# One kernel, three edits around the modulation vectors: VectorE alone for the second group, in-projections' norm without GpSimd, the first group ahead of most filter spectra

## The chip, the cores and the metric

The kernel runs on one core of a Trainium2 chip. The metric is the device time of one execution in microseconds (us); the median of three executions of the kernel before is 1859.73 us (1854.02 to 1862.49). Five engines matter: TensorE (PE, with its weight loads PEld), VectorE (DVE), ScalarE (ACT), GpSimd (POOL) and SyncE (SP), which issues nearly all of the DMAs.

## The reference, cut to what matters

Two layers of a diffusion transformer over 512 latent tokens and 256 context tokens, model width 1024. Each layer reads six modulation vectors per stream (latent, context), normalises, projects in, runs three kinds of token mixing side by side (Hyena convolution, neighbourhood attention NA, latent attention MLA), projects out, and runs an MLP of width 4096.

```python
def _modulation(cond, w_mod, b_mod):
    m = jax.nn.silu(cond) @ w_mod + b_mod
    return jnp.split(m[:, None, :], 6, axis=-1)
def _adaln(h, g, shift, scale):
    return _rms(h, g) * (1.0 + scale) + shift
for i in range(DEPTH):
    mx = _modulation(c, w_mod[i], b_mod[i])            # latent; mc: the same with c_ctx
    px = _adaln(x, g_norm1[i], mx[0], mx[1]) @ w_in[i]
    ...                                                 # Hyena (filters made from hy_f_*), NA, MLA
    x = x + mx[2] * (mix @ w_out[i])
    x = x + mx[5] * _sqrelu_mlp(_adaln(x, g_norm2[i], mx[3], mx[4]), ...)
```

## The kernel before, in words

Activations are kept feature-major: 128 partitions, eight blocks k of the width, 768 tokens (latent 0 to 511, context 512 to 767). Every product is made of three matmuls, each operand being split into a high and a low part (`split`, lines 134 to 137: the high part by an ACT copy on L136, the low part by a DVE subtraction on L137). Weights of the big GEMMs stream from HBM in blocks of 512 KB through the SP queue into a ring of three raw buffers, and each block is split into `wh` and `wl` (`wblock`; its DMA is L280). A GEMM (L295) works through eight k of an output block m.

Modulation vectors (l, v), v = 0 to 5, are made in two ways. `modulation` does it on PE: eight weight tiles `wm` [128, 1024] of `w_mod`, four matmuls each (L150), a transpose (L158). `modulation_rows` does it without PE: per vector eight items, each a tile `wm` of `w_modr` that is multiplied by the row of activated conditions and summed along the row. In the kernel before POOL multiplies by the context's row (L189), ACT sums that product (L194), and DVE multiplies by the latent's row and sums (L193). Vectors (0,1) and (0,0) are made by `modulation` at the start, (0,2) and (0,4) by `modulation` during layer 0's MLA attention, and (0,3), (0,5) and all six of layer 1 by `modulation_rows` during layer 0's out-projection and MLP (64 items).

The order of work is that of the program, in which generators are woven (`weave` with a rate for each, `fill` for work that is slipped in between matmuls); a scheduler of the framework then moves instructions on each engine's queue, except the DMAs of `w_modr`, which keep their order (`pin`). At run time each engine takes its queue strictly in order. During out-projection and MLP one item of `modulation_rows` is issued per output block m or hidden block; the table `FR` gives the number per hidden block in the first two of the MLP's four groups.

At the start SP loads the inputs, the sixteen `w_mod` tiles and the first weights, while PE also makes the Hyena filters' spectra: L357 and L372 (L335 and L350 after the change) compute the filter network, L392 and L401 its norms, L409 (L387) the transform. The first norm multiplies x by the reciprocal norm `rb` (`norm_x`), then `norm_h` makes the high part on ACT, the full value on DVE (L253) and the low part by a subtraction on POOL (L254). Layer 1 does the same per stream (`norm_stream`, L263 to L266), between the MLA in-projection (L295) and the NA value projection (`na_v`, L131 to L133). Out-projection is L1370, the gated residual add L1059, the split of the next input L1375 and L1376, the sum of squares L216 and L217, its reduction over partitions L224 (PE).

Lines of the kernel after stand 22 lines lower in number from the projection code on (before's L1059 is L1037 there), and the two multiplies of an item are L191.

Of the kernel before, what the change touches and what calls it, by code (L numbers as in the profile page):

```python
# [15 lines left out]
AF = mybir.ActivationFunctionType  # L16
# [20 lines left out]
def r32(ap):  # L37
    return ap.bitcast(F32)
# [3 lines left out]
def kernel(ctx, tc, A, dbg=None, stop=None):  # L42
# [131 lines left out]
    def modulation_rows(lv, cr, p):  # L174

        items = [(l, v, k) for l, v in lv for k in range(KD)]
        W, P = {}, {}
        def item(i):
            return items[i] if 0 <= i < len(items) else None

        for i in range(len(items) + MD + 2):
            if item(i):
                l, v, k = items[i]
                W[i] = p([128, 1024], tag="wm", bufs=3)
                pin(sp.dma_start(W[i], A["w_modr"][l, v, k]))
            if item(i - MD):
                l, v, k = items[i - MD]
                P[i - MD] = p([128, 1024], tag="wmp", bufs=2)
                pool.tensor_tensor(P[i - MD], W[i - MD], cr[:, 1], ALU.mult)  # L189
            if item(i - MD - 1):  # L190
                l, v, k = items[i - MD - 1]  # L191
                pr, w = P.pop(i - MD - 1), W.pop(i - MD - 1)
                dve.scalar_tensor_tensor(w, w, 1.0, cr[:, 0], ALU.mult, ALU.mult, accum_out=mods[:, l, v, k, 0:1])  # L193
                act.activation(pr, pr, AF.Copy, accum_out=mods[:, l, v, k, 1:2])  # L194
            if item(i - MD - 2) and items[i - MD - 2][2] == KD - 1:
                l, v, k = items[i - MD - 2]
                bm = cols[:, l, C_BMOD + v * 8:C_BMOD + v * 8 + 8]
                dve.tensor_add(mods[:, l, v], mods[:, l, v], bm.unsqueeze(2).to_broadcast([128, KD, 2]))
                if v % 3 == 1:
                    gain(l, v // 3)  # L200
            yield
# [37 lines left out]
    def norm_x(xT, rb, nt):
        for k in range(KD):  # L240
            dve.tensor_mul(xT[:, k, :nt], xT[:, k, :nt], rb)
            yield
        yield

    def norm_h(l, n, xT, hh, hl, nt, p):

        streams = [e for e in STREAM if e[1] < nt]
        for k in range(KD):
            t = p([128, nt], tag="sq", bufs=2)
            for s, a, b in streams:  # L250
                g, m = gains[:, l, n, k, s:s + 1], mods[:, l, 3 * n, k, s:s + 1]
                act.activation(hh[:, k, a:b], xT[:, k, a:b], AF.Identity, bias=m, scale=g)
                dve.tensor_scalar(t[:, a:b], xT[:, k, a:b], g, m, ALU.mult, ALU.add)  # L253
            pool.tensor_sub(hl[:, k, :nt], t, r32(hh[:, k, :nt]))  # L254
            yield

    def norm_stream(l, s, rb, xT, hh, hl, p):

        _, a, b = STREAM[s]
        for k in range(KD):  # L260
            t = p([128, NT], tag="sq", bufs=2)[:, a:b]
            g, m = gains[:, l, 0, k, s:s + 1], mods[:, l, 0, k, s:s + 1]
            dve.tensor_mul(xT[:, k, a:b], xT[:, k, a:b], rb[:, a:b])  # L263
            act.activation(hh[:, k, a:b], xT[:, k, a:b], AF.Identity, bias=m, scale=g)
            dve.tensor_scalar(t, xT[:, k, a:b], g, m, ALU.mult, ALU.add)
            pool.tensor_sub(hl[:, k, a:b], t, r32(hh[:, k, a:b]))  # L266


    nw = [0]
# [26 lines left out]
                                  stop=(k == nk - 1 and i == 2))  # L296
                next(fill, None)

    MD = 1
    EA = 8  # L300
    MF, VF = 0.5, 0.4

# [11 lines left out]
    NSB, NPT = 3, 4  # L314
    MB = 4
    EM = 8
    FR = (0, 2)


    kx = [tc.dram_tile([128, 2, 2, 2, 2, 256], F32, name=f"kx{l}") for l in range(DEPTH)]  # L320
# [636 lines left out]
    def mla_attend(l, qrs, qk0, qkd, vd, mh, ml, p):  # L957
# [8 lines left out]
        def heads_in(h):  # L966

            hp, z = divmod(h, 2)
            if z == 0 and hp:
                QK[hp] = p([128, 2, 6, 192], tag="qk", bufs=2)  # L970
                for e, n in ((0, nq), (1, 6)):
                    sp.dma_start(QK[hp][:, e, 0:n], qkd[hp, :, e, 0:n])
            if hp:
                q, k = [QK[hp][:, e, :, 96 * z:96 * z + 96] for e in range(2)]
            else:
                q, k = qk0[z]
            qh, ql = p([96, NT], F32R, tag="qh", bufs=3), p([96, NT], F32R, tag="ql", bufs=3)
# [12 lines left out]
            T[h] = ((qh, ql), (kh, kl))  # L990
# [92 lines left out]
    def mlp(l, xT, hh, hl, rstd, streams, p, tail, fill=iter(())):  # L1083
# [10 lines left out]
        def ff1(c):  # L1094
            nonlocal rb
            ah, al = p([128, 4, n], F32R, tag="ah", bufs=2), p([128, 4, n], F32R, tag="al", bufs=2)
            ts = {}
            for j in range(4):
                f = 4 * c + j
                if f == 0:  # L1100
                    ts = {i: (mm_tile(), wblock(A["w_ff1"][l, i])) for i in range(2)}
                    gemm([ts[0][0], ts[1][0]], [ts[0][1], ts[1][1]], KD, (hh, hl), [rng, rng], fill=early())
                    rb = next(rstd)
                    ts[2] = (mm_tile(),)
                    gemm(ts[2][0], wblock(A["w_ff1"][l, 2]), KD, (hh, hl), rng)
# [14 lines left out]
                for s, a, b in STREAM[:len(streams)]:  # L1120
                    act.activation(r[:, a:b], r[:, a:b], AF.Relu, bias=bb[:, s:s + 1])
                dve.tensor_mul(r, r, r)  # L1122
                split(ah[:, j], al[:, j], r)
                for _ in range(FR[c] if c < 2 else 1):
                    next(fill, None)
            return ah, al

# [31 lines left out]
    def chain(*gs):  # L1159
        for g in gs:  # L1160
            yield from g
# [26 lines left out]
    def x_in():
        for rb in rstd:
            yield  # L1190
        for _ in zip(*[norm_x(xT, rb, NT)] * 3):
            yield
# [16 lines left out]
    sc = Pool("norm0", "right")  # L1209
    rstd = norm_rstd(acc, NT, sc)  # L1210
    fill = spectra()
    weave((x_in(), 1.0), (chain(modulation(0, 1, wmp, ws=wm1), modulation(0, 0, wmp, ws=wm0)), 1.0), fill=(fill, 1.4))
    wmp.close()
    sc.close()
    hp_ = Pool("h0")
    hh, hl = hp_([128, KD, NT], F32R), hp_([128, KD, NT], F32R)
    cp = Pool("c0")
    cqh, cql, ssq = cp([128, 3, NT], F32R), cp([128, 3, NT], F32R), cp([128, 2, 6])
    for _ in norm_h(0, 0, xT, hh, hl, NT, xp):
        pass  # L1220
    xp.close()

    xd = tc.dram_tile([128, KD, S], F32, name="x_spill")
    qkd = [tc.dram_tile([4, 128, 2, 6, 192], F32, name=f"qk_spill{l}") for l in range(DEPTH)]
# [2 lines left out]
    for l in range(DEPTH):  # L1227
# [4 lines left out]
        if l:  # L1232
# [332 lines left out]
```

## Time and profile before

| what | us |
|---|---|
| median of three executions | 1859.73 |
| the profiled execution | 1861.99 |
| its span in the trace | 1860.1 |
| PE busy | 1770.8 (95%) |
| DVE busy | 1227.3 (66%) |
| ACT busy | 807.1 (43%) |
| POOL busy | 339.4 (18%) |

The profiled execution is one execution with the hardware profiler. A busy time is the union of the engine's instructions. A matmul of 512 columns in float32 shows as two records; the number of records in a stretch says how dense PE is, even where its busy time is full.

### The profile page before, as it was taken

Reading aid. Unit: us, or ns where it says so; the run is one execution under the profiler, and the core shown is the slowest. Engines: PE = TensorE matmul, PEld = TensorE weight load, DVE = VectorE, ACT = ScalarE, POOL = GpSimd, SP = SyncE. Lnnn points to the kernel's source line nnn. Section 1 sums busy time; section 2 is a strip of 40 time slices with the busy share of each in tenths; the row PEclk is TensorE's granted clock in tenths of the full one; section 3 lists DMA queues with packets and bytes.
Section 4 is the critical chain, followed back from the end, with each engine's and each line's share of the span. In section 5 each row is a group of like instructions: output and inputs, shape, how many; then the busy total and the mean of one; then the engine's idle time right before and its main releaser. Section 6 shows DMA issues by size and latency. Waiting matters only on the chain. (4 is left out here: it accounts for less than half of the span.)

```text
span 1860.1 us, 27267 instructions
## 1 busy us (share of the span) xinstructions
PE 1770.8 (95%) x10794; PEld 1504.4 (81%) x10794; DVE 1227.3 (66%) x2111; ACT 807.1 (43%) x1355; POOL 339.4 (18%) x265
## 2 busy tenths in 40 slices
PE   6899988899998999999999999899899999999999
PEld 2688877666686878888888888789677799999997
DVE  5866876766668876665666447887876665555554
ACT  3433425566644643334333224554566652333231
POOL 1523321200043433233322000530300000000000
PEclk9999998999998999999999999899999999999999
DMA  9123423151243333333332222363040023223332
GB/s 339 60 85 134 161 95 101 42 207 56 100 160 126 114 136 130 120 114 136 113 136 102 69 68 88 96 202 132 24 177 24 24 93 100 91 91 95 98 91 79
DMA packets 73246, 205.07 MB, mean 110 GB/s; under 512 B 12540, under 2 KB 24589, under 8 KB 71840
## 3 DMA queue, kind: packets, MB, share of 16 engines
q1 hardware_dynamic: 71520, 198.10, 31.0%
q0 software_dynamic: 1600, 5.24, 0.8%
q8 instruction: 85, 1.39, 0.3%
q14 instruction: 41, 0.34, 0.1%
HBM read 181.30 MB, written 21.23 MB: 109 GB/s over the span
## 5 line engine op out<-in xcount | busy, mean ns | idle before, releaser
L295 PE MATMUL mm<-t,wh 128*128 128x512 f32 (+1 forms) x2496 | 495.2, 319 | 1.9 <-DVE t L1059 1.3
L295 PEld LDWEIGHTS mm<-t,wh 128*128 128x128 f32 x2496 | 373.2, 190 | 38.0 <-issue 2.4
L136 ACT ACTIVATE wh<-wr 128x1024 fp32r<-128x1024 f32 (+2 forms) x176 | 184.6, 1050 | 415.8 <-PE mm L295 394.4
L295 PE MATMUL mm<-t,wl 128*128 128x512 f32 (+1 forms) x1248 | 298.1, 317 | 0.0
L189 POOL TENSOR_TENSOR wmp<-wm,t 128x1024 f32<-128x1024 f32 x64 | 169.5, 2655 | 485.8 <-DMA wm<-in_w_modr_dram 308.8
L137 DVE TENSOR_TENSOR wl<-wr,wh 128x1024 fp32r<-128x1024 f32 (+2 forms) x176 | 228.0, 1296 | 37.3 <-ACT wh L136 33.8
L295 PE MATMUL mm<-ah,wh 128*128 128x512 f32 (+1 forms) x768 | 231.4, 355 | 4.1 <-DVE t L1059 3.5
L295 PE MATMUL mm<-al,wh 128*128 128x512 f32 (+1 forms) x768 | 233.5, 359 | 0.0
L295 PE MATMUL mm<-ah,wl 128*128 128x512 f32 (+1 forms) x768 | 232.0, 356 | 0.0
L1059 DVE SCALAR_TENSOR_TENSOR t<-mm,mods,t 128x512 f32<-128x512 f32 x216 | 135.9, 657 | 134.3 <-PE mm L295 127.5
L295 PEld LDWEIGHTS mm<-t,wl 128*128 128x128 f32 x1248 | 194.7, 189 | 16.5
L193 DVE SCALAR_TENSOR_TENSOR wm<-wm,t 128x1024 f32<-128x1024 f32 x64 | 91.0, 1426 | 102.7 <-POOL wmp L189 102.7
L295 PEld LDWEIGHTS mm<-ah,wh 128*128 128x128 f32 x768 | 126.7, 188 | 28.5 <-DVE t L1059 3.4
L295 PEld LDWEIGHTS mm<-ah,wl 128*128 128x128 f32 x768 | 127.6, 188 | 22.4
L295 PEld LDWEIGHTS mm<-al,wh 128*128 128x128 f32 x768 | 126.4, 188 | 20.2
L194 ACT ACTIVATE wmp<-wmp 128x1024 f32<-128x1024 f32 x64 | 67.9, 1060 | 149.8 <-POOL wmp L189 149.8
L137 DVE TENSOR_TENSOR al<-relu,ah 128x768 fp32r<-128x768 f32 (+1 forms) x64 | 68.2, 1066 | 37.1 <-ACT ah L136 37.1
L447 DVE TENSOR_REDUCE mmx<-mm 128x1 f32<-128x768 f32 (+1 forms) x80 | 67.7, 847 | 32.1 <-PE mm L133 31.5
L452 ACT ACTIVATE msb<-mm,mmx,qrs 128x768 f32<-128x768 f32 (+1 forms) x80 | 72.2, 903 | 25.3 <-DVE mmx L449 21.3
L1370 PE MATMUL mm<-t,wh 128*128 128x512 f32 x320 | 78.1, 358 | 1.6 <-DVE t L1059 1.6
L1023 ACT ACTIVATE mpt<-mm 128x768 f32<-128x768 f32 (+1 forms) x80 | 57.5, 725 | 49.7 <-PE mm L1022 49.6
L136 ACT ACTIVATE ah<-relu 128x768 fp32r<-128x768 f32 (+1 forms) x64 | 47.3, 739 | 63.4 <-DVE relu L1122 63.3
(311 smaller groups left out, 2990.1 us busy)
## 6 DMA issues: line engine op xcount, KB each, us to landing
wr<-in_w_ff_dram SPq DMA_DIRECT2D x128, 512.0 KB, 3.5
wm<-in_w_modr_dram SPq DMA_DIRECT2D x64, 512.0 KB, 4.4
wm<-in_w_mod_dram SPq DMA_DIRECT2D x32, 512.0 KB, 8.0
wr<-in_w_in_t_dram SPq DMA_DIRECT2D x18, 512.0 KB, 3.8
qk<-qk_spill SPq DMA_DIRECT2D x9, 576.0 KB, 6.2
qk_spill<-upk SPq DMA_DIRECT2D x12, 384.0 KB, 3.0
kx<-kk POOLq DMA_DIRECT2D x16, 256.0 KB, 2.5
wr<-in_w_in_qk_dram SPq DMA_DIRECT2D x8, 512.0 KB, 4.0
```

What stands on the lines that cost most here:

```text
L136: act.activation(hi, src, AF.Copy)
L137: dve.tensor_sub(lo, src, r32(hi))
L189: pool.tensor_tensor(P[i - MD], W[i - MD], cr[:, 1], ALU.mult)
L193: dve.scalar_tensor_tensor(w, w, 1.0, cr[:, 0], ALU.mult, ALU.mult, accum_out=mods[:, l, v, k, 0:1])
L194: act.activation(pr, pr, AF.Copy, accum_out=mods[:, l, v, k, 1:2])
L295: pe.matmul(out_[:, po:po + b - a], wk[wx], mk[mx][:, a:b], start=(k == 0 and i == 0), stop=(k == nk - 1 and i == 2))
L447: dve.tensor_reduce(mx, src, AX.X, ALU.max, negate=True)
L452: act.activation(sb[:, h, :n], src[:, h, :n], AF.Exp, bias=mx[:, h:h + 1], scale=1.0 if scale is None else scale[:, h:h + 1], accum_out=sm ...
L1023: act.activation(pt[:, 0:nkt, qt * 128:(qt + 1) * 128], tt[:, :nkt * 128].rearrange("p (c q) -> p c q", q=128), AF.Copy)
L1059: dve.scalar_tensor_tensor(xT[:, m, a:b], t[:, a:b], mods[:, l, v, m, s:s + 1], xT[:, m, a:b], ALU.mult, ALU.add)
L1370: pe.matmul(t[:, a:b], ws[wx], half[mx][:, k % 4, a:b], start=(k == ks[0] and i == 0), stop=(k == 7 and i == 2))
```

## The change

`modulation_rows` keeps its weight tiles and their DMAs, but both products are made by DVE, with two `scalar_tensor_tensor` with accumulation per item; weights are loaded two items ahead (`MD` 2) instead of one. Vector (0,3) moves from the out-projection into layer 0's MLA attention, with conditions loaded and activated for it once more; `FR` becomes one item per hidden block from the second group on, none in the first; the three `next(fill)` behind the out-projection go. The ring `qk` of the MLA attention has one buffer instead of two, in both layers. `norm_x` and `norm_h` go; both layers use `norm_stream`, which multiplies on DVE, applies gain and shift on ACT in place, and splits with ACT and DVE. At the start the first modulation is woven with half as much spectral work per step as the spectra's former rate (0.5 instead of 1.4), and `rb` is made behind it.

```diff
+        for i in range(MD):
+            weights(i)
+        for i, (l, v, k) in enumerate(items):
+            weights(i + MD)
+            w, junk = W.pop(i), p([128, 1024], tag="wmp")
+            for s in range(2):
+                dve.scalar_tensor_tensor(w if s else junk, w, 1.0, cr[:, s], ALU.mult, ALU.mult,
+                                         accum_out=mods[:, l, v, k, s:s + 1])
-                pool.tensor_tensor(P[i - MD], W[i - MD], cr[:, 1], ALU.mult)
...
-                dve.scalar_tensor_tensor(w, w, 1.0, cr[:, 0], ALU.mult, ALU.mult, accum_out=mods[:, l, v, k, 0:1])
-                act.activation(pr, pr, AF.Copy, accum_out=mods[:, l, v, k, 1:2])
...
     def norm_stream(l, s, rb, xT, hh, hl, p):
         _, a, b = STREAM[s]
         for k in range(KD):
-            dve.tensor_mul(xT[:, k, a:b], xT[:, k, a:b], rb[:, a:b])
-            act.activation(hh[:, k, a:b], xT[:, k, a:b], AF.Identity, bias=m, scale=g)
-            dve.tensor_scalar(t, xT[:, k, a:b], g, m, ALU.mult, ALU.add)
-            pool.tensor_sub(hl[:, k, a:b], t, r32(hh[:, k, a:b]))
+            t, g, m = xT[:, k, a:b], gains[:, l, 0, k, s:s + 1], mods[:, l, 0, k, s:s + 1]
+            dve.tensor_mul(t, t, rb[:, a:b])
+            act.activation(t, t, AF.Identity, bias=m, scale=g)
+            split(hh[:, k, a:b], hl[:, k, a:b], t)
+            yield
...
-    MD = 1
+    MD = 2
-    FR = (0, 2)
+    FR = 1
-                QK[hp] = p([128, 2, 6, 192], tag="qk", bufs=2)
+                QK[hp] = p([128, 2, 6, 192], tag="qk")
-    weave((x_in(), 1.0), (chain(modulation(0, 1, wmp, ws=wm1), modulation(0, 0, wmp, ws=wm0)), 1.0), fill=(fill, 1.4))
+    next(fill)
+    next(rstd)
+    weave((chain(modulation(0, 1, wmp, ws=wm1), modulation(0, 0, wmp, ws=wm0)), 1.0), fill=(fill, 0.5))
+    rb = next(rstd)
...
+    for _ in zip(norm_stream(0, 0, rb, xT, hh, hl, xp), norm_stream(0, 1, rb, xT, hh, hl, xp)):
+        pass
...
-                  (chain(*[modulation(0, v, wmp) for v in (2, 4)]), 0.2))
+                  (chain(*[modulation(0, v, wmp) for v in (2, 4)]), 0.2),
+                  (modulation_rows([(0, 3)], cond_rows(wmp), wmp), 0.2))
...
-            fill = modulation_rows([(0, 3), (0, 5)] + [(1, v) for v in range(6)], cond_rows(wmp), wmp)
+            fill = modulation_rows([(0, 5)] + [(1, v) for v in range(6)], cond_rows(wmp), wmp)
...
-            for _ in range(MD + 2):
-                next(fill)
```

On VectorE, between the eighth blocks of the out-projection, the queue before reads as follows (L193 the latent's multiply, L1059 the gated add, L1376 the low part of the next input, L217 the sum of squares, L137 a weight block's low part).

```order
L193 SCALAR_TENSOR_TENSOR wm_5490,mods<-wm_5490,t_5011 128x1024
L1376 SCALAR_TENSOR_TENSOR t_5007<-t_5000,gains,t_5006 128x512
L1376 SCALAR_TENSOR_TENSOR t_5007<-t_5000,gains,t_5006 128x256
L217 TENSOR_TENSOR t_5001<-t_5001,sq_5277 128x768
L193 SCALAR_TENSOR_TENSOR wm_5560,mods<-wm_5560,t_5011 128x1024
L193 SCALAR_TENSOR_TENSOR wm_5566,mods<-wm_5566,t_5011 128x1024
L198 TENSOR_TENSOR mods<-mods,cols 128x16
L137 TENSOR_TENSOR t_5007<-mods,t_5006 128x8x2
L193 SCALAR_TENSOR_TENSOR wm_5572,mods<-wm_5572,t_5011 128x1024
L1059 SCALAR_TENSOR_TENSOR t_5000<-mm_5292,mods,t_5000 128x512
L1059 SCALAR_TENSOR_TENSOR t_5000<-mm_5292,mods,t_5000 128x256
L137 TENSOR_TENSOR wl_5498<-wr_5496,wh_5497 128x1024
```

After the change the same queue, at the end of the out-projection, reads so (L191 the two multiplies of an item, then the same operations 22 or 24 lines lower).

```order
L1352 SCALAR_TENSOR_TENSOR t_5059<-t_5052,gains,t_5058 128x256
L214 TENSOR_TENSOR t_5053<-t_5053,sq_5543 128x768
L191 SCALAR_TENSOR_TENSOR wmp_6056,mods<-wm_5615,t_5063 128x1024
L191 SCALAR_TENSOR_TENSOR wm_5615,mods<-wm_5615,t_5063 128x1024
L191 SCALAR_TENSOR_TENSOR wmp_6125,mods<-wm_5985,t_5063 128x1024
L1037 SCALAR_TENSOR_TENSOR t_5052<-mm_5557,mods,t_5052 128x512
L1037 SCALAR_TENSOR_TENSOR t_5052<-mm_5557,mods,t_5052 128x256
L137 TENSOR_TENSOR wl_5776<-wr_5774,wh_5775 128x1024
L1352 SCALAR_TENSOR_TENSOR t_5059<-t_5052,gains,t_5058 128x512
L1352 SCALAR_TENSOR_TENSOR t_5059<-t_5052,gains,t_5058 128x256
L214 TENSOR_TENSOR t_5053<-t_5053,sq_5612 128x768
L191 SCALAR_TENSOR_TENSOR wm_5985,mods<-wm_5985,t_5063 128x1024
```

The multiplies stand in pairs, or a block's work apart, and each first one of a pair waits for its own weights from DMA instead of for POOL.

On PE at the start, the stretch before the first GEMM (L295) reads as follows in the kernel before (L372 filter network, L150 modulation, L158 its transpose, L392, L401 and L409 spectra; names are tiles).

```order
L372 MATMUL b_461<-w_3_132,t_96 128x512
L150 MATMUL b_375<-wm_168,cst 32x256 x4
L150 MATMUL b_375<-wm_170,cst 32x256 x4
L372 MATMUL b_481<-w_3_132,t_96 128x512
L158 MATMUL b_491<-ident,wr_489 128x128 x2
L392 MATMUL b_496<-ones,facc_342 128x1 x4
L372 MATMUL b_506<-w_3_132,t_96 128x512
L401 MATMUL b_515<-ident,rnb_502 128x128 x2
L409 MATMUL b_520<-sd_343,t_136 128x256
```

In the kernel after, the corresponding stretch, up to its first GEMM matmul (L273), reads so.

```order
L150 MATMUL b_324<-wm_168,cst 32x256 x4
L150 MATMUL b_324<-wm_170,cst 32x256 x4
L158 MATMUL b_381<-ident,wr_379 128x128 x2
L370 MATMUL b_386<-ones,facc_231 128x1 x4
L232 MATMUL b_397<-ident,rs_253 128x128 x4
L232 MATMUL b_403<-ident,rs_253 128x128 x2
L350 MATMUL b_523<-w_3_132,t_96 128x512
L379 MATMUL b_544<-ident,rnb_392 128x128 x2
L387 MATMUL b_549<-sd_232,t_136 128x256
```

Ahead of the first GEMM, PE's queue before held ten rows of L372 and 24 of L409; after, it holds six of L350 and five of L387. The rest stands behind the first GEMM's beginning.

On SP, at the start of layer 0's MLA attention, the loads before were these (`qk` the queries and keys of a pair of heads, `wm` from `w_mod` for PE's modulation).

```order
L142 DMA wm_3636<-in_w_mod_dram 128x1024
L142 DMA wm_3642<-in_w_mod_dram 128x1024
L972 DMA qk_3758<-qk_spill_602 128x1152 x2
L142 DMA wm_3826<-in_w_mod_dram 128x1024
L142 DMA wm_3832<-in_w_mod_dram 128x1024
```

After, the loads of the vector (0,3) (`w_modr`) stand among them.

```order
L183 DMA wm_3659<-in_w_modr_dram 128x1024
L183 DMA wm_3661<-in_w_modr_dram 128x1024
L950 DMA qk_3778<-qk_spill_486 128x1152 x2
L183 DMA wm_3663<-in_w_modr_dram 128x1024
L142 DMA wm_3846<-in_w_mod_dram 128x1024
```

The load of the next heads now waits for the only `qk` buffer, and the loads behind it in the queue wait with it.

## Rows read from the trace of the kernel before

**Rows 1.** The page's busy times: engine, busy us (share of span), instructions.
```profile
PE 1770.8 (95%) x10794; PEld 1504.4 (81%) x10794; DVE 1227.3 (66%) x2111; ACT 807.1 (43%) x1355; POOL 339.4 (18%) x265
```

**Rows 2.** Windows: length, busy (count) of PE, PEld, DVE, ACT, POOL; clock, DMA share, GB/s.
```profile
560.00:570.00 10.00, 10.00 (x58) 8.69 (x57) 10.00 (x8) 2.57 (x5) 6.89 (x3) 1.00 0.26 95
570.00:580.00 10.00, 6.43 (x26) 5.07 (x25) 9.71 (x16) 6.38 (x11) 2.37 (x1) 0.76 0.31 105
580.00:590.00 10.00, 10.00 (x54) 8.72 (x53) 7.32 (x11) 5.51 (x8) 0.00 (x0) 0.89 0.52 175
590.00:600.00 10.00, 6.28 (x36) 5.24 (x34) 7.23 (x8) 4.16 (x7) 4.75 (x2) 0.96 0.13 52
600.00:610.00 10.00, 8.50 (x32) 7.65 (x33) 5.70 (x9) 2.30 (x4) 4.68 (x2) 0.53 0.36 143
670.00:680.00 10.00, 8.86 (x48) 7.24 (x48) 6.17 (x8) 4.50 (x8) 2.50 (x1) 1.00 0.58 196
680.00:690.00 10.00, 7.08 (x39) 5.99 (x40) 9.60 (x13) 4.37 (x6) 2.40 (x1) 1.00 0.09 29
```

**Rows 3.** Timeline of PE in these windows: start, us, then idle before and releaser.
```profile
601.50 2.72 PE L224 MATMUL b<-ones,t 128*128 128x1 f32 x12 [5.22 <-DVE t L217]
...
682.47 0.62 PE L295 MATMUL mm<-ah,wh 128*128 128x512 f32 x2 [3.07 <-DVE t L1059]
```

**Rows 4.** POOL's group by line: busy us, mean ns | idle before, what ended it.
```profile
L189 POOL TENSOR_TENSOR wmp<-wm,t 128x1024 f32<-128x1024 f32 x64 | 169.5, 2655 | 485.8 <-DMA wm<-in_w_modr_dram 308.8
```

**Rows 5.** Timeline of DVE in the out-projection, same columns as Rows 3.
```profile
558.32 3.42 DVE L193 SCALAR_TENSOR_TENSOR wm<-wm,t 128x1024 f32<-128x1024 f32 x1
...
577.00 0.94 DVE L217 TENSOR_TENSOR t<-t,sq 128x768 f32<-128x768 f32 x1
577.87 1.21 DVE L193 SCALAR_TENSOR_TENSOR wm<-wm,t 128x1024 f32<-128x1024 f32 x1
...
579.01 1.13 DVE L1059 SCALAR_TENSOR_TENSOR t<-mm,mods,t 128x512 f32<-128x512 f32 x2
580.07 1.21 DVE L137 TENSOR_TENSOR wl<-wr,wh 128x1024 fp32r<-128x1024 f32 x1
581.20 1.14 DVE L1376 SCALAR_TENSOR_TENSOR t<-t,gains,t 128x512 fp32r<-128x512 f32 x2
...
592.77 3.41 DVE L193 SCALAR_TENSOR_TENSOR wm<-wm,t 128x1024 f32<-128x1024 f32 x1 [5.45 <-POOL wmp L189]
```

**Rows 6.** PE's waits by releaser: us in total, times, longest.
```profile
PE mm L133 <- POOL t L266: 4.2, 4, 2.3
...
PE mm L131 <- ACT t L264: 1.3, 1, 1.3
```

**Rows 7.** A window of layer 1's in-projection, columns as in Rows 2.
```profile
1180.00:1190.00 10.00, 7.55 (x34) 7.09 (x34) 10.00 (x18) 6.99 (x12) 6.55 (x8) 0.66 0.00 1
```

**Rows 8.** A window at the start, columns as in Rows 2.
```profile
45.00:50.00 5.00, 4.28 (x19) 2.77 (x20) 4.43 (x7) 1.17 (x3) 0.19 (x1) 1.00 0.02 7
```

**Rows 9.** Timeline of PE at the start, columns as in Rows 3.
```profile
36.60 1.08 PE L150 MATMUL b<-wm,cst 128*32 128x256 f32 x8
37.62 2.07 PE L372 MATMUL b<-w,t 65*128 65x512 f32 x2
...
57.24 1.02 PE L372 MATMUL b<-w,t 65*128 65x512 f32 x2
...
59.20 3.72 PE L409 MATMUL b<-sd,t 128*128 128x256 f32 x16
...
75.51 1.05 PE L295 MATMUL mm<-t,wh 128*128 128x512 f32 x4
...
162.91 0.98 PE L295 MATMUL mm<-t,wh 128*128 128x512 f32 x4 [0.54 <-ACT t L489]
```

**Rows 10.** A window of layer 0's MLA attention, columns as in Rows 2.
```profile
430.00:450.00 20.00, 19.27 (x137) 13.18 (x137) 13.12 (x35) 13.56 (x29) 0.00 (x0) 1.00 0.10 27
```

**Rows 11.** DMA issues: engine, count, KB each, us to landing.
```profile
wm<-in_w_modr_dram SPq DMA_DIRECT2D x64, 512.0 KB, 4.4
```

More of the change, by code (lines that the diff above doesn't have):

```diff
@@ L176, in modulation_rows, with weights @@
         items = [(l, v, k) for l, v in lv for k in range(KD)]
[L177 to L182, printed above, removed]
+        W = {}
+        def weights(i):
+            if i < len(items):
                 l, v, k = items[i]
@@ L185, in modulation_rows @@
                 pin(sp.dma_start(W[i], A["w_modr"][l, v, k]))
-            if item(i - MD):
-                l, v, k = items[i - MD]
-                P[i - MD] = p([128, 1024], tag="wmp", bufs=2)
-                pool.tensor_tensor(P[i - MD], W[i - MD], cr[:, 1], ALU.mult)
-            if item(i - MD - 1):
-                l, v, k = items[i - MD - 1]
-                pr, w = P.pop(i - MD - 1), W.pop(i - MD - 1)
-                dve.scalar_tensor_tensor(w, w, 1.0, cr[:, 0], ALU.mult, ALU.mult, accum_out=mods[:, l, v, k, 0:1])
-                act.activation(pr, pr, AF.Copy, accum_out=mods[:, l, v, k, 1:2])
-            if item(i - MD - 2) and items[i - MD - 2][2] == KD - 1:
-                l, v, k = items[i - MD - 2]
+        for i in range(MD):
[6 more added lines that the diff above has]
+                                         accum_out=mods[:, l, v, k, s:s + 1])
+            if k == KD - 1:
                 bm = cols[:, l, C_BMOD + v * 8:C_BMOD + v * 8 + 8]
@@ L237, in norm_rstd @@
         yield rb
[L239 to L251, printed above, removed]
-                act.activation(hh[:, k, a:b], xT[:, k, a:b], AF.Identity, bias=m, scale=g)
-                dve.tensor_scalar(t[:, a:b], xT[:, k, a:b], g, m, ALU.mult, ALU.add)
-            pool.tensor_sub(hl[:, k, :nt], t, r32(hh[:, k, :nt]))
-            yield
     def norm_stream(l, s, rb, xT, hh, hl, p):
@@ L260, in norm_stream @@
         for k in range(KD):
-            t = p([128, NT], tag="sq", bufs=2)[:, a:b]
-            g, m = gains[:, l, 0, k, s:s + 1], mods[:, l, 0, k, s:s + 1]
-            dve.tensor_mul(xT[:, k, a:b], xT[:, k, a:b], rb[:, a:b])
-            act.activation(hh[:, k, a:b], xT[:, k, a:b], AF.Identity, bias=m, scale=g)
-            dve.tensor_scalar(t, xT[:, k, a:b], g, m, ALU.mult, ALU.add)
-            pool.tensor_sub(hl[:, k, a:b], t, r32(hh[:, k, a:b]))
+            t, g, m = xT[:, k, a:b], gains[:, l, 0, k, s:s + 1], mods[:, l, 0, k, s:s + 1]
[3 more added lines that the diff above has]
+            yield
     nw = [0]
@@ L1123, in ff1 @@
                 split(ah[:, j], al[:, j], r)
-                for _ in range(FR[c] if c < 2 else 1):
+                for _ in range(FR if c else 0):
                     next(fill, None)
@@ L1186 @@
     hid.close()
[L1188 to L1192, printed above, removed]
     def spectra():
@@ L1211 @@
     fill = spectra()
-    weave((x_in(), 1.0), (chain(modulation(0, 1, wmp, ws=wm1), modulation(0, 0, wmp, ws=wm0)), 1.0), fill=(fill, 1.4))
+    next(fill)
+    next(rstd)
+    weave((chain(modulation(0, 1, wmp, ws=wm1), modulation(0, 0, wmp, ws=wm0)), 1.0), fill=(fill, 0.5))
+    rb = next(rstd)
     wmp.close()
-    sc.close()
     hp_ = Pool("h0")
     hh, hl = hp_([128, KD, NT], F32R), hp_([128, KD, NT], F32R)
+    for _ in zip(norm_stream(0, 0, rb, xT, hh, hl, xp), norm_stream(0, 1, rb, xT, hh, hl, xp)):
+        pass
+    sc.close()
+    xp.close()
     cp = Pool("c0")
     cqh, cql, ssq = cp([128, 3, NT], F32R), cp([128, 3, NT], F32R), cp([128, 2, 6])
-    for _ in norm_h(0, 0, xT, hh, hl, NT, xp):
-        pass
-    xp.close()
     xd = tc.dram_tile([128, KD, S], F32, name="x_spill")
@@ L1239 @@
             sc = Pool(f"mlain{l}", "right")
-            late = norm_rstd(acc, NT, sc), lambda s, rb: norm_stream(l, s, rb, xT, hh, hl, xp)
+            late = norm_rstd(acc, NT, sc), lambda s, rb: list(norm_stream(l, s, rb, xT, hh, hl, xp))
         if l:
@@ L1378 @@
             next(fill, None)
-        if not last:
-            for _ in range(MD + 2):
-                next(fill)
         split(hh[:, :, nt:nt + 2], hl[:, :, nt:nt + 2], mods[:, l, 3])
```

## The prediction

> **What bounds the kernel now.** The first view is the page's table of busy times: PE has 95% of the span, DVE 66%, ACT 43%, POOL 18% [rows 1]. Only PE can set the end, so a change is worth what it takes out of PE's empty or slow time, and nothing else: 1860.1 minus 1770.8 leaves 89 us of idle, plus what is lost at the lower clock. The second view is the windows, where the reader should look at the count of PE's records beside its busy time. A dense stretch of a GEMM has 58 in 10 us [rows 2]. In the four windows from 570 to 610, end of layer 0's out-projection and the norm behind it, there are 26, 54, 36 and 32, 148 in all for 232 that would fit: 84 missing at 5.8 per us are 14.5 us. From 670 to 690 there are 87 for 116: 5.0 us. These 19.5 us are the largest stake. The third view, PE's timeline, says who is late: PE idles 5.22 us until DVE's sum of squares and 3.07 us until its gated add [rows 3].
>
> Why DVE is late is in two more views. POOL's multiplies take 2.66 us each, and POOL idled 308.8 us for their weights [rows 4]. In DVE's timeline one and the same multiply takes 1.21 us at 577.87, where POOL's column is empty, and 3.42 us at 558.32; at 592.77 DVE had stood 5.45 us waiting for POOL's product and then took 3.41 [rows 5]. So DVE pays twice for POOL: about 2.2 us where both run, and a wait in its queue, behind which the gated adds and sums of squares stand that PE waits for.
>
> **Out-projection and MLP of layer 0.** Removed: 64 POOL multiplies, 64 ACT sums, 64 DVE multiplies. Added: two DVE multiplies per item at 1.21 us plus little for reading the sum, 2.5 us. One output block m with one item then costs DVE 1.21 (weight split) + 1.13 (gated add) + 1.14 (low part) + 0.94 (sum of squares) + 2.5 = 6.9 us [rows 5], while PE needs 24 matmuls over 768 columns, about 49 records at 5.8 per us, 8.5 us [rows 2]. The order puts not eight but twelve items between the out-projection's beginning and the rstd (24 rows of L191), so DVE has 8 x 4.4 + 12 x 2.5 = 65 us of work for 68 us of PE. That is nearly full, but without the lock, and all but the last two blocks have slack. A new wait: the first multiply of a pair now waits for DMA itself, and the weights of the ninth and tenth item stand on SP behind MLP blocks that wait for weight splits. A landing takes 4.4 us [rows 11], and the scheduler has put 3.6 to 4.7 us of DVE work between, so I take 1 us of wait for each, ahead of the last gated add. Of the 14.5 us I take 12.5 to go; bounds 0 (DVE as late as now) and 14.5. The 5.0 us at 670 to 690 fall where each hidden block had two items; there is one now, since eight items left for the MLA attention: all 5.0, bounds 2 and 5. Beyond 700 PE is dense already, and 1.2 us more DVE per item hides under PE. Sum −17, bounds −2 to −19.5.
>
> **Layer 1's in-projection.** POOL's subtractions go; PE's waits for them and for the high part are 4.2 + 1.3 us [rows 6], and the clock fell to 0.66 in 1180 to 1190, where 34 matmuls of 288 columns ran at half speed for about 6 us, 2.7 us lost [rows 7]. What is late next: ACT has two passes per k instead of one, and the order puts na_v's second group, whose context rows need these passes, ahead of the first group's last k, because the third weight block is split only behind the whole norm. The eight context steps then end at about the time at which they ended before. I take −2, with bounds −8 (all gone) and +3 (an ACT chain of 16 x 1.4 us is later than POOL's was by that).
>
> **Start.** Here instructions only move. Before the first GEMM, at 75.51, PE computed ten L372 and 24 L409; now six and five. Moved behind it are 4 x 1.0 us, 19 x 0.465 us (16 records, eight matmuls, take 3.72) and about 1 us of norms: 13.8 us, and the distance from first GEMM to Hyena's in-projection, 162.91 − 75.51 = 87.4 us, becomes 101 [rows 9]. When does the first GEMM start? All its weights have landed by 45: the DMA share is 0.02 after that [rows 8]. PE has, at the slow pace of these rows, 6 x 2.07 + 16 x 1.08 us for spectra and modulation, 2.9 + 2.7 + 1.4 + 1.5 + 2.5 + 4.6 for the rest, 45.4 us from 17.7 on: 63, with small waits 65. If PE runs at the full clock from about 40 on, it waits for weights and for the norm's first step (a multiply, two ACT passes, a subtraction, some 4.5 us), and starts at about 53. The same L372 row takes 2.07 at 37.62 and 1.02 at 57.24 [rows 9], so the pace is open by a factor of two; the clock column reads 1.00 all along and does not help. So Hyena's in-projection starts at 154 to 166 against 162.91: −9 to +3. I take −5, since most modulation steps wait for the DMA and not for PE's pace.
>
> The Trainium skill, in "TensorE: Matmul & The Clock Gate", section "HAM oscillation", says that a loop whose short bursts of matmuls are divided by waits for DMA falls back to the lower clock between the bursts, so that each burst starts cold. By it the start stays slow until 65, and the term is +3 instead of −5; the trace agrees for the kernel before (2.07 us until about 51) and can't say it for the new order.
>
> **Layer 0's MLA attention.** Added are 16 DVE multiplies (16 x 1.3 = 21 us), eight loads, a second load and activation of the conditions on ACT, and one `qk` buffer fewer. PE is dense here (19.27 of 20 us), DVE has 13.12 of 20 and ACT 13.56 [rows 10]. Over the 100 us in which the items lie DVE goes from 66 to 87%: there is room on the mean, but the softmax's steps queue behind a pair of 2.5 us. PE has eight heads' work in flight; I take +3, bounds 0 and +12. In layer 1 the single `qk` buffer delays loads that are needed some 15 us later: 0, bounds 0 and +3.
>
> **Sum.** −17 − 2 − 5 + 3 = −21 from the profiled execution's 1861.99 gives 1841. The median of the runs is 2.3 lower, so 1839.
>
> **Rivals.** (1) Cold start: all as above, but the first GEMM at 65: 1839 + 8 = 1847. For it: rows of 2.07 us until the weights are in, and fewer matmuls to keep PE at work. Against: modulation is then nearly contiguous. (2) DVE is the bound of the out-projection: 65 of 68 us of work is no slack once weights come late, and PE waits for adds as it did. Only half of the 17 us goes: 1839 + 9 = 1848, up to 1856 if none goes. For it: SP's order as above; against: the lock, 2.2 us per overlap, is certainly gone. (3) Slower: in the MLA attention a multiply that heads DVE's queue waits for its weights, whose load stands on SP behind a `qk` load that waits for the only buffer. A landing of 4.4 us and the pair's 2.5 us, exposed on PE for all eight items, are 8 x 6.9 = 55 us: 1839 − 3 + 55 = 1891. It decides from 24 / 8 = 3 us of PE wait per item on. For it: PE waits for DVE's softmax wherever it is late, and DVE is strictly in order; against: two loads are ahead, and DMA is at a tenth here. (4) The change does less than it says, since POOL's lock never was on PE's path from 570 on: then −2 to −5 in all, 1855 to 1858; the 5.45 us behind POOL's product speaks against it.
>
> **Numbers.** Forecast 0.60 (own range 1829 to 1849), rival 1 0.17, rival 2 0.10, rival 3 0.07, rival 4 0.06. Half a percent, 9.3 us, is about what a measurement of this kernel can tell from no change: below 1850.4 is faster, above 1869 slower. Faster: 0.60 + 0.14 + 0.06 = 0.80; slower 0.07; same 0.13. The terms at their good ends give 1859.7 − 19.5 − 8 − 9 = 1823; upward 1858 takes in rivals 1, 2 and most of 4.
>
> **What would show it.** In the profile after: 55 records or more in every 10 us from out-projection to the first hidden blocks, and every DVE multiply at 1.2 us. A first GEMM between 53 and 58, and the filter network's matmuls at 1.0 us from about 45, for the start. In the MLA attention no wait of PE above 3 us for the softmax. The prediction is wrong if PE still misses over 8 us around the norm behind the out-projection, if the attention grew by more than 12 us, or if layer 1's na_v has new waits for ACT above 5 us.

## The result, and the profile after

The kernel after takes 1833.56 us (median; 1831.39 to 1838.49) against 1859.88 us beside it: a ratio of 0.9863, 95% interval 0.9842 to 0.9884, 26.3 us less. 1839 with 1823 to 1858 was forecast. Timed again on another chip the ratio was 0.9860 (0.9825 to 0.9895).

The spans of the two profiles differ by 28.4 us. Cut at the same matmuls in both traces, this is where they lie:

| stretch (from its first matmul to the next's) | before | after | change | forecast |
|---|---|---|---|---|
| start to layer 0's Hyena in-projection | 162.9 | 151.1 | −11.9 | −5 |
| from there to layer 0's MLA attention | 211.9 | 212.4 | +0.5 | 0 |
| layer 0's MLA attention | 136.0 | 145.2 | +9.2 | +3 |
| out-projection and MLP, to layer 1's in-projection | 649.2 | 628.4 | −20.8 | −17 |
| layer 1's in-projection to the end of na_v | 38.0 | 36.3 | −1.7 | −2 |
| from there to the last MLA up-projection | 43.6 | 38.9 | −4.7 | 0 |
| the rest | 618.5 | 619.4 | +0.9 | 0 |

The profiled sum came out 7 us below the forecast's −21: three gains were larger, one loss too. Two of the terms left their own bounds: the start (−9 to +3) and out-projection and MLP (−2 to −19.5). First the page of after, busy time by engine, to be put beside [rows 1]:

```profile
PE 1752.5 (96%) x10794; PEld 1499.4 (82%) x10794; DVE 1233.4 (67%) x2247; ACT 754.7 (41%) x1262; POOL 135.8 (7%) x177
```

POOL lost 204 us and ACT 52, but DVE gained only 6 us for 64 more multiplies: what they cost was given back, most of it by instructions that no longer run slowed. Two groups of before (busy us, mean ns of one, idle before and releaser), then three of after, say so:

```profile
L137 DVE TENSOR_TENSOR wl<-wr,wh 128x1024 fp32r<-128x1024 f32 (+2 forms) x176 | 228.0, 1296 | 37.3 <-ACT wh L136 33.8
...
L193 DVE SCALAR_TENSOR_TENSOR wm<-wm,t 128x1024 f32<-128x1024 f32 x64 | 91.0, 1426 | 102.7 <-POOL wmp L189 102.7
```

```profile
L137 DVE TENSOR_TENSOR wl<-wr,wh 128x1024 fp32r<-128x1024 f32 (+2 forms) x176 | 214.1, 1217 | 30.5 <-ACT wh L136 27.1
...
L191 DVE SCALAR_TENSOR_TENSOR wmp<-wm,t 128x1024 f32<-128x1024 f32 x64 | 78.3, 1224 | 68.3 <-DMA wm<-in_w_modr_dram 68.3
...
L191 DVE SCALAR_TENSOR_TENSOR wm<-wm,t 128x1024 f32<-128x1024 f32 x64 | 78.1, 1220 | 0.2
```

Every multiply takes 1.22 us, where [rows 5] had 1.21 and 3.42. DVE now waits for DMA, 68.3 us in all, where POOL did [rows 4]; the windows of the out-projection and the MLP's first blocks show that PE does not notice (busy and record counts, clock third from the end):

```profile
540.00:550.00 10.00, 10.00 (x59) 8.68 (x58) 10.00 (x18) 2.92 (x4) 0.00 (x0) 1.00 0.49 161
550.00:560.00 10.00, 10.00 (x59) 8.69 (x58) 9.60 (x14) 2.92 (x4) 0.00 (x0) 1.00 0.46 157
560.00:570.00 10.00, 10.00 (x59) 8.63 (x57) 9.55 (x18) 3.67 (x5) 0.00 (x0) 1.00 0.52 159
570.00:580.00 10.00, 10.00 (x59) 8.70 (x58) 9.34 (x15) 4.37 (x8) 0.00 (x0) 1.00 0.32 105
580.00:590.00 10.00, 10.00 (x63) 8.93 (x62) 7.04 (x18) 7.18 (x14) 0.00 (x0) 1.00 0.31 107
590.00:600.00 10.00, 10.00 (x61) 8.81 (x60) 5.02 (x12) 5.20 (x9) 0.00 (x0) 1.00 0.16 49
600.00:610.00 10.00, 10.00 (x59) 8.77 (x58) 9.62 (x15) 5.46 (x9) 0.00 (x0) 1.00 0.50 168
660.00:670.00 10.00, 10.00 (x59) 8.73 (x58) 6.77 (x11) 1.06 (x1) 0.00 (x0) 1.00 0.45 150
670.00:680.00 10.00, 10.00 (x58) 8.70 (x57) 5.97 (x10) 1.06 (x1) 0.00 (x0) 1.00 0.43 156
```

No window has under 58 records, where [rows 2] had 26, 36 and 32. In the attention it is the other way round. Two windows of before, 20 us behind its first matmul, then those of after, from its first matmul on:

```profile
395.00:415.00 20.00, 20.00 (x148) 12.78 (x147) 12.49 (x33) 12.92 (x25) 0.00 (x0) 1.00 0.39 138
415.00:435.00 20.00, 20.00 (x130) 13.85 (x130) 13.74 (x35) 13.52 (x25) 0.00 (x0) 1.00 0.18 55
```

```profile
364.00:384.00 20.00, 14.79 (x91) 11.54 (x89) 15.75 (x28) 15.92 (x21) 0.00 (x0) 0.83 0.50 197
384.00:404.00 20.00, 17.62 (x130) 13.09 (x130) 16.89 (x38) 11.80 (x22) 0.00 (x0) 0.91 0.67 228
404.00:424.00 20.00, 18.94 (x119) 11.29 (x116) 15.90 (x39) 10.20 (x23) 0.00 (x0) 1.00 0.64 204
424.00:444.00 20.00, 17.32 (x123) 12.23 (x122) 16.40 (x41) 12.99 (x23) 0.00 (x0) 1.00 0.26 85
444.00:464.00 20.00, 20.00 (x127) 13.91 (x127) 13.47 (x36) 14.31 (x29) 0.00 (x0) 1.00 0.29 100
```

While items last (to 438) DVE is at 15.8 to 16.9 of 20 us and PE below 19; behind them PE is full again. In before PE has 20 us in both windows shown, with DVE at 12.5 to 13.7; its first 20 us are short there too (16.2 of 20, at a clock of 0.91). The start, PE's timeline of after:

```profile
42.06 3.23 PE L150 MATMUL b<-wm,cst 128*32 128x256 f32 x56
45.86 0.44 PE L158 MATMUL b<-ident,wr 128*128 128x128 f32 x2 [0.56 <-ACT wr L155]
...
48.53 1.81 PE L350 MATMUL b<-w,t 65*128 65x512 f32 x2 [0.74 <-ACT rb L233]
...
53.38 1.39 PE L273 MATMUL mm<-t,wh 128*128 128x512 f32 x6
...
151.06 0.97 PE L273 MATMUL mm<-t,wh 128*128 128x512 f32 x4 [0.53 <-ACT t L467]
```

Seven modulation steps run in 3.23 us, 0.46 each, less than half of the 1.08 that the same eight records took in [rows 9], and the first GEMM starts at 53.38, the warm end of the forecast. PE was slow once more at 48.53, where L350 takes 1.81 us again, behind small matmuls and a wait of 0.74 us; the granted clock is 0.88 in 45 to 50 and 0.77 in 50 to 55.

### The profile page after: what moved, and what is told of

Read it like the earlier page. It is cut to its first block, busy times and chain, and to the rows that moved or that the text cites. A ratio compares the mean times of both kernels' runs of the same rounds, so it can differ in the third digit from the quotient of the medians.

```text
span 1831.7 us, 27057 instructions
## 1 busy us (share of the span) xinstructions
PE 1752.5 (96%) x10794; PEld 1499.4 (82%) x10794; DVE 1233.4 (67%) x2247; ACT 754.7 (41%) x1262; POOL 135.8 (7%) x177
## 5 line engine op out<-in xcount | busy, mean ns | idle before, releaser
L273 PE MATMUL mm<-t,wh 128*128 128x512 f32 (+1 forms) x2496 | 492.5, 317 | 1.9 <-DVE t L1037 1.3
L273 PEld LDWEIGHTS mm<-t,wh 128*128 128x128 f32 x2496 | 371.4, 189 | 37.9 <-issue 1.9
L273 PE MATMUL mm<-t,wl 128*128 128x512 f32 (+1 forms) x1248 | 296.9, 316 | 0.0
L137 DVE TENSOR_TENSOR wl<-wr,wh 128x1024 fp32r<-128x1024 f32 (+2 forms) x176 | 214.1, 1217 | 30.5 <-ACT wh L136 27.1
L273 PE MATMUL mm<-al,wh 128*128 128x512 f32 (+1 forms) x768 | 233.6, 359 | 0.0
L273 PE MATMUL mm<-ah,wl 128*128 128x512 f32 (+1 forms) x768 | 232.2, 356 | 0.0
L273 PE MATMUL mm<-ah,wh 128*128 128x512 f32 (+1 forms) x768 | 230.9, 354 | 0.0
L273 PEld LDWEIGHTS mm<-t,wl 128*128 128x128 f32 x1248 | 193.6, 189 | 16.2 <-DVE wl L137 0.2
L273 PEld LDWEIGHTS mm<-ah,wl 128*128 128x128 f32 x768 | 127.6, 188 | 22.5
L273 PEld LDWEIGHTS mm<-ah,wh 128*128 128x128 f32 x768 | 126.7, 188 | 23.6
L273 PEld LDWEIGHTS mm<-al,wh 128*128 128x128 f32 x768 | 126.3, 188 | 20.1
L191 DVE SCALAR_TENSOR_TENSOR wmp<-wm,t 128x1024 f32<-128x1024 f32 x64 | 78.3, 1224 | 68.3 <-DMA wm<-in_w_modr_dram 68.3
L1090 DVE TENSOR_SCALAR bb<-mm,cols 128x2 f32<-128x2 f32 x64 | 14.0, 219 | 97.6 <-PE mm L273 97.4
L191 DVE SCALAR_TENSOR_TENSOR wm<-wm,t 128x1024 f32<-128x1024 f32 x64 | 78.1, 1220 | 0.2
L137 DVE TENSOR_TENSOR al<-relu,ah 128x768 fp32r<-128x768 f32 (+1 forms) x64 | 52.6, 823 | 36.2 <-ACT ah L136 36.1
```

The costliest lines, as they stand in the source:

```text
L137: dve.tensor_sub(lo, src, r32(hi))
L191: dve.scalar_tensor_tensor(w if s else junk, w, 1.0, cr[:, s], ALU.mult, ALU.mult, accum_out=mods[:, l, v, k, s:s + 1])
L273: pe.matmul(out_[:, po:po + b - a], wk[wx], mk[mx][:, a:b], start=(k == 0 and i == 0), stop=(k == nk - 1 and i == 2))
```

## The experiments

All were timed in five rounds beside the kernel before. Stretches in the texts below are those of the table, from one profiled execution each.

**Multiplies by VectorE alone, weights two items ahead (e1_rows_dve).**

```diff
 kernel before
-    pool.tensor_tensor(P[i - MD], W[i - MD], cr[:, 1], ALU.mult)   # and ACT's sum
+    for s in range(2): dve.scalar_tensor_tensor(w if s else junk, w, 1.0, cr[:, s], ...)
-    MD = 1
+    MD = 2
```

> The kernel before with one edit: both multiplies of an item by VectorE, weights loaded two items ahead; vector (0,3) stays in the out-projection, two items per hidden block in the MLP's second group, and the three items behind the out-projection stay. Theory A (GpSimd's lock and the wait for its product made VectorE late): the stalls from 570 to 610 and 670 to 690 go though the item count is as before, -14 to -20 us against before. Theory B (the stalls come from too many items at these places, whoever makes them): VectorE has 1.2 us more per item, the stalls stay, -3 to +5 us.

1841.19 us against 1861.53, ratio 0.9883 (0.9864 to 0.9901), −20.3 us. Out-projection and MLP take 625.6 us, 23.7 less than before; the other stretches together take 4 more. With more items than after, VectorE full and PE never short (windows of this run):

```profile
560.00:580.00 20.00, 20.00 (x115) 17.36 (x114) 19.55 (x34) 6.06 (x9) 0.00 (x0) 1.00 0.49 157
580.00:600.00 20.00, 20.00 (x120) 17.64 (x119) 18.21 (x36) 4.52 (x6) 0.00 (x0) 1.00 0.64 202
600.00:620.00 20.00, 20.00 (x117) 17.53 (x116) 19.80 (x36) 16.81 (x31) 0.00 (x0) 1.00 0.48 160
```

DVE is busy 18.2 to 19.8 of 20 us, fuller than before, and the stall is gone. Theory A holds, B falls. What the longer lead of the weights gives and what GpSimd's absence gives, this run does not part.

**GpSimd back, with the fewer items of after (e7_pool_rows).**

```diff
 kernel after
-    fill = modulation_rows([(0, 5)] + ...)
+    fill = modulation_rows_p([(0, 5)] + ...)      # the form of the kernel before
```

> The kernel after, but with GpSimd, ScalarE and VectorE making the products again (as before, weights one item ahead) in out-projection and MLP; (0,3) stays in the attention by VectorE, so that the item count is that of after. Theory A: most of the 20.8 us between out-projection and the end of the MLP comes back, +12 to +20 us against after. Theory B: the place is smooth since eight items left, +0 to +5 us.

1840.67 us against 1861.53, 0.9888 (0.9868 to 0.9907): −20.9 us, about 5 less gain than after had, and the intervals overlap; in the profiles out-projection and MLP take 4.6 us more than in after. That is the upper end of theory B; A's 12 to 20 us did not come. Out-projection to the MLP's second half takes 138.9 us (first matmul of the second MLP product), as in after and e1 and not 154.7 as before; only the 5 us behind it are back (494.1 us, before 494.5, after 489.5), though at another place: one wait of 2.9 us for VectorE at 659, where [rows 3] has the one for the gated add at 682. DVE's timeline shows that slowed multiply and wait are still there:

```profile
556.59 3.43 DVE L219 SCALAR_TENSOR_TENSOR wm<-wm,t 128x1024 f32<-128x1024 f32 x1
...
581.15 1.23 DVE L219 SCALAR_TENSOR_TENSOR wm<-wm,t 128x1024 f32<-128x1024 f32 x1 [5.44 <-POOL wmp L215]
```

So the big stall needed both, the form with GpSimd and the items of (0,3) at that place; either cure alone removes it. With (0,3) went the three `next(fill)`: in the 91 us from the out-projection's first matmul to where before stalled for its sum of squares VectorE starts 10 of these multiplies in e7 and 13 in before. The small stall needs the form with GpSimd only.

**The new start alone (e4_start).**

```diff
 kernel before
-    weave((x_in(), 1.0), (chain(modulation(0, 1, ...), modulation(0, 0, ...)), 1.0), fill=(fill, 1.4))
+    next(fill); next(rstd)
+    weave((chain(modulation(0, 1, ...), modulation(0, 0, ...)), 1.0), fill=(fill, 0.5))
+    rb = next(rstd)      # and the in-place norm for layer 0
```

> The kernel before with the new start alone (first modulation ahead of most spectra, in-place norm without GpSimd for layer 0's in-projection). The traces of before and after show Hyena's in-projection 12 us earlier. If this is the order alone, -11 to -13 us against before, and the first GEMM at 53; if another part helped there, less than -8.

1852.72 us against 1861.53, 0.9951 (0.9933 to 0.9969), −8.8 us; the first GEMM at 53.2, the first MLA up-projection at 159.4, as in after (53.4, 159.5) and not as in before (75.5, 171.5). In the profile the start gives the whole 12 us, and the other stretches together take 4 more; the time lies between the two expectations. The edit holds the new order and the norm without GpSimd together, and no run parts them.

**Layer 1's norm alone (e5_norm1).**

```diff
 kernel before, norm_stream of layer 1
-    act.activation(hh, xT, AF.Identity, bias=m, scale=g); dve.tensor_scalar(t, xT, g, m, ...)
-    pool.tensor_sub(hl, t, hh)
+    act.activation(t, t, AF.Identity, bias=m, scale=g); split(hh, hl, t)
```

> The kernel before with one edit: layer 1's norm by VectorE and ScalarE, without GpSimd. The traces of before and after differ by 1.7 us up to the end of na_v and by another 4.7 us in the Hyena in-projection behind it. Theory A (both come from this norm): -5 to -7 us against before. Theory B (only na_v's part does): -1 to -3 us.

1853.79 us against 1861.53, 0.996 (0.9944 to 0.9976), −7.7 us. na_v ends after 37.9 us (before 38.0), and the stretch behind it takes 38.8 (before 43.6); together that is 4.9 of the 7.7 us. The two stretches have to be read together, since a piece of work changed sides: matmuls of one column each (`csq`, 28 records) stand behind na_v in before and amid it in e5 and after. Before:

```profile
1198.84 3.18 PE L673 MATMUL b<-ones,csq 128*128 128x1 f32 x28
1201.88 0.70 PE L295 MATMUL mm<-t,wh 128*128 128x512 f32 x2
...
1204.62 1.05 PE L295 MATMUL mm<-t,wh 128*128 128x512 f32 x2
```

e5:

```profile
1180.81 5.97 PE L672 MATMUL b<-ones,csq 128*128 128x1 f32 x28
```

So about 3 of the 4.8 us behind na_v are this work moved. na_v took it in, at 5.8 us, and is no longer than before: its own matmuls are through 5.9 us sooner. PE's waits in the two stretches tell why, first before, then e5:

```profile
PE mm L133 <- POOL t L266: 4.2, 4, 2.3
PE mm L131 <- ACT t L264: 1.3, 1, 1.3
PE mm L132 <- DVE wl L137: 1.2, 1, 1.2
```

```profile
PE mm L131 <- ACT t L136: 2.9, 1, 2.9
```

Of 6.7 us of waits 2.9 are left. Another 1.7 us are a second fall of the clock in before, [rows 7] being the first. Windows of before and of e5, both among matmuls of 512 columns:

```profile
1203.00:1208.00 5.00, 5.00 (x17) 3.94 (x16) 4.18 (x17) 1.06 (x1) 3.95 (x14) 0.66 0.66 225
```

```profile
1203.00:1208.00 5.00, 5.00 (x25) 4.35 (x25) 3.15 (x4) 3.68 (x6) 3.09 (x11) 1.00 0.76 230
```

PE has no idle time in either, but 17 records against 25, at a clock of 0.66 against 1.00; the GEMM of 24 matmuls that the fall hits takes 7.17 us in before and 5.49 in e5 and after. Theory A holds by the time and for the stretch behind na_v; the 1.7 us up to na_v's end did not come here (0.1).

All four kernels with GpSimd in this norm (before, e1, e4, e6) take 41.9 to 45.2 us for the stretch behind na_v, all that leave it out 38.8 or 38.9. In three of the four the clock falls there (that GEMM takes 7.17, 8.44 and 8.17 us); in e6 it does not (5.57 us), though the same 28 records of small matmuls stand ahead of it. What decides was not tried and stays open.

**Vector (0,3) back in the out-projection (e2_03_back).**

```diff
 kernel after
-                  (modulation_rows([(0, 3)], cond_rows(wmp), wmp), 0.2))
-            fill = modulation_rows([(0, 5)] + ...)
+            fill = modulation_rows([(0, 3), (0, 5)] + ...)
-    FR = 1
+    FR = (0, 2)
```

> The kernel after with vector (0,3) back in the out-projection (both multiplies by VectorE), two items per hidden block in the MLP's second group as before; the rest is after's. The single parts measured so far (-20.3, -8.8 and -7.7 us) sum to -36.8 us, 10 more than the whole change. Theory A (the move of (0,3) into the attention costs this): the attention is as short as before, 1861.5 - 37 = 1825 us. Theory B (the parts overlap elsewhere): about 1834 us, as after.

1821.13 us against 1862.97, 0.9788 (0.9761 to 0.9815), −41.8 us: the lowest ratio of all, and its interval lies below after's. The attention takes 134.9 us, while out-projection and MLP stay at 628.4. Theory A holds; the move bought nothing and cost about 10 us in the profile, 14 by the ratios.

**One qk buffer, alone (e6_qk1).**

```diff
 kernel before
-                QK[hp] = p([128, 2, 6, 192], tag="qk", bufs=2)
+                QK[hp] = p([128, 2, 6, 192], tag="qk")
```

> The kernel before with one edit: one qk buffer instead of two in the MLA attention of both layers. If the 9.2 us that layer 0's attention lost come from the load of the next heads being late: +5 to +9 us against before; if from what was added to ScalarE and VectorE: 0 to +1 us.

1856.64 us against 1862.97, 0.9975 (0.9956 to 0.9995). Neither expectation came: −6.3 us. The attention takes 132.0 us, 4 less than before, so the buffer isn't the cost. The first 20 us run at a clock of 1.00 where before had 0.91, with a first wait of 1.3 us for the softmax instead of 2.5. That the buffer brings this is not shown: e2 has one buffer too, and its first 20 us run at 0.83.

**No activation of rows (e3_rows_dram).**

```diff
 kernel after
-        cr = load(p, "cond_rows", [128, 2, 1024]); act.activation(cr, cr, AF.Silu)
+        cr = load(p, None, [128, 2, 1024], cd.to_broadcast([128, 2, 1024]))
+    for s in range(2): sp.dma_start(cd[0, s].rearrange("(k q) -> q k", q=128), cst[:, :, s])
```

> The kernel after, but the activated conditions go from the tile that the start makes through a small DRAM tile and come back as rows, so that both activations of rows with their table loads fall away. Theory A (the activation and two table loads at the beginning of the MLA attention, 4.5 us of ScalarE, hold up the first softmax and let the clock fall): -3 to -5 us against after's 1833.6. Theory B (VectorE's multiplies in the softmax's queue cost it): 0 to -1 us.

1847.61 us against 1862.97, 0.9921 (0.9901 to 0.9942): −15.4 us, 11 less gain than after had. In the profile the loss lies at the start (first up-projection at 173.1, 13.6 us later than in after): the small DMA, 2048 elements of 4 bytes, went between the modulation's and the first GEMM's weights, and in 45 to 50 the queues were busy at 46 GB/s with PE at 1.08 of 5 us:

```profile
45.00:50.00 5.00, 1.08 (x8) 0.20 (x8) 0.00 (x0) 0.00 (x0) 0.29 (x1) 0.86 0.86 46
```

The attention still takes 145.2 us. Its first wait was 3.9 us for ACT in after and is 3.0 us for DVE here: theory A falls, and the time missed both.

**Its combination with e2 and two buffers (e8_best).** The edits of e2 and e3, and `bufs=2` for `qk`.

> e2_03_back with two qk buffers and the conditions by DRAM as in e3_rows_dram, so that out-projection has no activation of rows either. A version that should beat both: 1825 us by theory A of e2_03_back, and 0 to 2 us less for the activation (4.5 us of ScalarE in the out-projection, where it is idle).

1840.2 us against 1862.97, 0.9881 (0.9859 to 0.9903): a miss by 15 us against the expected 1825. The same 15 us are lost at the start (first up-projection at 174.3, in e2 at 159.3), the attention takes 136.0, and no gain from the missing activation is seen.

**After again, with the multiplies cut to 16 columns (so that (0,3) is left incomplete), and with half the rate (a0_after, e9_thin, e10_slow).**

```diff
 kernel after, the (0,3) items in the attention: e9
-    dve.scalar_tensor_tensor(w, w, 1.0, cr[:, s], ...)
+    dve.scalar_tensor_tensor(w[:, 0:16], w[:, 0:16], 1.0, cr[:, s, 0:16], ...)
 e10
-    (modulation_rows([(0, 3)], cond_rows(wmp), wmp), 0.2)
+    (modulation_rows([(0, 3)], cond_rows(wmp), wmp), 0.1)
```

> The kernel after itself, timed on the chip beside the next two: 1831 to 1836 us, layer 0's attention (first transpose of qk to first matmul of the out-projection) 145 us as in its first profile.

> The kernel after, but the sixteen multiplies of vector (0,3) in the attention take only the first 16 of 1024 columns, so that (0,3) is not the reference's; loads, waits, activation and buffers stay. Theory A (VectorE's time for the multiplies, in the softmax's queue): the attention falls from 145 to 135 to 137 us, -8 to -10 us against after. Theory B (the waits for weights that came later, or the queue of loads): it stays at 143 to 145 us.

> The kernel after with the items of (0,3) woven at half the rate (0.1 instead of 0.2), so that they are spread over nearly the whole attention. Theory A1 (VectorE is full in the first 75 us and has room later): attention 139 to 141 us, -4 to -6 us against after. Theory A2 (every multiply delays a softmax by a fixed part, 10 / 16 = 0.6 us, wherever it stands): 144 to 146 us, no change.

a0 1837.98, e9 1827.05, e10 1832.13 us against 1866.28; ratios 0.986 (0.9825 to 0.9895), 0.9803 (0.9771 to 0.9836) and 0.9833 (0.9801 to 0.9865); a0 is 2 us above its expected range, on a chip on which before is slower too. The attention: 145.1, 136.4 and 141.6 us. With the same loads, waits, activation and buffers, taking away only VectorE's time takes away 8.7 of the 9.2 us: A holds against B. Spreading the items gives back 3.5 us of the profile's stretch, just short of A1's 4 to 6 and far from A2's nothing. The waits of e9 still hold the activation's,

```profile
PE mm L1026 <- ACT msb L456: 3.9, 1, 3.9
```

and e9's attention lies 1.5 us over that of e2, where there is none: the activation costs no more than about that once VectorE is free. In e10 the waits of PE are spread as well, 2.3 us in four for the softmax's maximum:

```profile
PE mm L1000 <- DVE mmx L427: 2.3, 4, 1.1
```

## Why the prediction was right, point by point

- **Out-projection and MLP** (−17 forecast, −20.8): right that VectorE was late and that POOL's part in the items made it so (e1: −20.3 us by this edit alone), and right that 65 us of VectorE's work fit beside PE: it ran at 9.5 to 10 of 10 us in 540 to 570 without a stall of PE. The forecast kept 2 us for waits for weights ahead of the last adds; none came. Up to the second MLP product the gain was 15.8 us, where 12.5 were taken and 14.5 were the bound.
- **The 5 us at 670 to 690**: the size was right and the reason wrong. The step said that they go because each hidden block has one item instead of two. In e1 two items stay and the 5 us go; in e7 one item is left and a stall of that size stays. It was the form with POOL.
- **Whether POOL alone was the cause at 570 to 610**: rival 4 said that the lock was not on PE's path. e7 shows half of it: lock and 5.44 us waits remain, yet PE has no stall there; with three multiplies fewer up to that point VectorE is done before PE needs it.
- **Start** (−5 forecast, −11.9, bound −9): the mechanism was right, the size was hedged between slow and fast and fell short. First GEMM 53.4, the fast end, so rival 1 did not come true: modulation was gathered into runs of 32 and 56 records. The first, at 30.58, still took 0.91 us a step at a granted clock of 0.50 (1.2 GHz); the long ones from 36 us on took 0.46 to 0.48 at 0.98 to 1.00. The distance from the first GEMM to the in-projection became 97.7 us, 3 less than the 101 worked out by moving 13.8 us of spectra. The rule that the prediction took from the Trainium skill ("TensorE: Matmul & The Clock Gate", section "HAM oscillation") is for bursts that are divided by waits for DMA. Neither trace has its case: PE waits 0.7 us in all between 30.6 and 45 in after, and in before, where the prediction saw agreement, it is busy for all of 30 to 40 while L372 takes 2.07 us.
- **Layer 1's in-projection** (−2 forecast, −6.4 in two stretches): the mechanism was right for na_v, POOL's waits went and one for ACT came (2.9 us), but the term was too small, and the −1.7 and −4.7 of the table do not part it, since the one-column matmuls moved across their border (e5). What the prediction did not look for is the second fall of the clock, 1.7 us in before.
- **MLA attention** (+3 forecast, +9.2, bound +12): the size that failed, three times too small. The step took room on the mean (87% of VectorE) for cover. e9 measures what it left out: 16 multiplies of 1.22 us are 19.5 us of queue, and 8.7 us of that reached PE. Rival 3 named the right stage, but not the cause: VectorE waited 1.3 us for these weights in all, not 4.4 per item, and the loss is 1.1 us per item where 3 were needed to turn the sign. The `qk` buffer costs nothing (e6). The sign set for this stage, no wait of PE above 3 us, failed: the first one is 3.9 us, for ACT.
- **Sum**: −21 forecast, −28.4 in the profiles, −26.3 in the medians. Three gains were too small by 15 us, one loss by 6, and 1.4 us lie in stretches that were forecast at nothing. That the time came within 5.4 us of 1839 is in part luck: misses of 15 and of 6 us have opposite signs. The best version is the change without its move (e2).

## What to carry to other kernels

When VectorE is late, ask first whether its instructions are long because GpSimd is at work: here the same multiply took 1.2 or 3.4 us, and giving VectorE more instructions and GpSimd none made it earlier. Work that hid beside a GEMM with VectorE at 9.5 to 10 of 10 us did not hide beside the softmax: there VectorE had a third of its time free on the mean, and 8.7 of 19.5 us added still reached PE. Measure the parts apart: two cures for one stall do not add up, and one part of a good change cost a third of it here.

## What was not expected of the hardware

PE slowed down without any idle time in the trace: in before at 1203 the granted clock fell to 0.66 and 5 us held 17 records of a kind of which e5 has 25 there; in e1 and e4 it fell to 0.50 with 13. A view of waits alone misses the 1.7 us that this costs in before and the 2.7 to 3 us in e1 and e4. A raw count of records misleads there too: in before the 5 us up to 1203 hold 41, but 28 of them are matmuls of one column.

And a DMA of 2048 single elements, 8 KB in all, was followed by late weights: the last tile of `w_mod` landed at 48.82 in e3 and at 42.48 in after, and the first weight block was split at 54.45 and at 45.70. The second block's split, at 71.61 in e3 and 48.37 in after, is not late by the DMA alone: ACT is busy with the norm without a break ahead of it, which after's order puts behind that split.
